# Two feed-forward norms through memory, and the last rows in tiles of 128 tokens

## The chip, the cores and the metric

The kernel runs on one core of one Trainium2 chip. The time is that of the device in microseconds; the kernel ran three times, and the median counts. Engines are called as in the profile: PE (TensorE), DVE (VectorE), ACT (ScalarE), POOL (GpSimd), SP (SyncE, which only issues transfers).

## The reference

The trunk has two layers over 512 tokens of 1024 features, float32. Layer 0 mixes tokens with a gated delta rule, layer 1 with latent attention. After each mixer comes a feed-forward network, and at the end one more norm:

```python
def rms_norm(x, gain):
    y = x * lax.rsqrt(jnp.mean(x * x, axis=-1, keepdims=True) + NORM_EPS)
    return y * gain

for i in range(2):
    x = x + mixer_i(rms_norm(x, norm_mix[i]))
    x = x + swiglu(rms_norm(x, norm_ffn[i]), w_gate_up[i], w_down[i])
return rms_norm(x, final_norm)

def swiglu(h, w_gate_up, w_down):      # 1024 -> 2 x 2816 -> 1024
    gu = h @ w_gate_up
    return (jax.nn.silu(gu[..., :D_FF]) * gu[..., D_FF:]) @ w_down
```

## The kernel before

**Layout.** Between the stages the tokens lie along the free axis: `xT` is 8 tiles of 128 features x 512 tokens. A dense product takes 128 columns of a weight matrix (a "unit", 512 KB, loaded by SP into `wst`). The unit is split into a high and a low part, `whi` (ACT, L122) and `wlo` (DVE, L123), in two halves of 128x512, and each of its eight slices is multiplied three times (`mm3`, L189 to L191), so 24 matmuls with 512 columns a unit. There is room for two split units and three loaded ones: a half of a unit is split when PE has used up the same half of the unit two before it.

**The feed-forward norm.** The factor of a token, 1/sqrt(mean of squares + eps), is not applied to the input of the network but to its products. While the gate and up products of the first of 22 feature tiles run on the tokens without their factor, the squares are already summed over the feature tiles in `acc`. `norm_scale` is called after the first gate and up product: `token_sum` (L209) sums `acc` over the partitions on PE, which leaves the sum of token t*128+p in partition p, column t; `rstd` computes the factor `r` (L202 on DVE, L203 on POOL, a power of -0.5). `spread` then makes `rb`, 128 partitions x 512 tokens with the factor of each token in every partition: DVE makes a diagonal matrix from `r` (L215), PE multiplies a matrix of ones with it (L218), ACT copies the result from PSUM (L220). `rb` is used at once: DVE multiplies the gate product by it (L861), ACT takes SiLU (L862), DVE multiplies by the up product (L863); then the result is split for the down product. L861 is also what frees the PSUM buffer of the gate product. The gate products use two buffers, `mm`; the up products use `st` and `sm` in turn. The down products use `rb` as well (L876). `norm_scale` runs twice, once in each layer; the norms of the attention call `spread` themselves.

**The end.** In the last layer, the down product of the last of eight feature tiles is taken by `last_rows` in two halves of 256 tokens. Its three weight units are split ahead. Behind each half the new `xT` is made (L907, L909), squared (L911) and multiplied by the gain (L913); PE sums the squares over the partitions for each of two tiles of 128 tokens (L917, L918) and turns the tile (L919); `rstd` makes the factor for both; DVE and ACT scale the rows in `y_rows` (L923 to L927), and SP and ACT send them, one 512 KB transfer for 128 tokens (L928).

**Order of the work.** The framework sets semaphores and orders the instructions of each engine itself: an instruction that its planner takes to be ready goes ahead of a waiting one of earlier code, so splits of later units stand between the steps of the norm. Each engine then executes in this order: whatever stands behind a waiting instruction waits as well. `after(first, then)` fixes the order of two instructions; `ordered` pins PE's order in the scan and the attention, not in the feed-forward networks.

Of the kernel before, what the change touches and what calls it, by code (L numbers as in the profile page):

```python
# [11 lines left out]
F32 = mybir.dt.float32  # L12
F32R = mybir.dt.float32r
I32 = mybir.dt.int32
AF = mybir.ActivationFunctionType
ALU = mybir.AluOpType
AX = mybir.AxisListType

P = 128
T = 512  # L20
D = 1024
# [29 lines left out]
def tile_trunk(ctx, tc, x, positions, norm_mix, norm_ffn, gdn_w_in, gdn_conv_w, gdn_a_log,  # L51
# [4 lines left out]
    act, dve, pe, pool, sync = nc.scalar, nc.vector, nc.tensor, nc.gpsimd, nc.sync  # L56
# [5 lines left out]
    sp = ctx.enter_context(tc.tile_pool(name="sp", bufs=2))  # L62
    pp = ctx.enter_context(tc.tile_pool(name="pp", bufs=2, space=bass.MemoryType.PSUM))
    dp = ctx.enter_context(tc.tile_pool(name="dp", bufs=1, space=bass.MemoryType.DRAM))
# [3 lines left out]
    def psum(tag, shape=(P, T)):  # L68
        return pp.tile(list(shape), F32, name="ps_" + tag, tag=tag, bufs=PS_BUFS[tag])

    def temp(shape, dtype=F32):
        return sp.tile(list(shape), dtype, name="temp", tag="t2", bufs=T2_BUFS)

    def slot(shape, tag, dtype=F32):
        return bp.tile(list(shape), dtype, name="slot_" + tag, tag=tag)


    ident = cp.tile([P, P], F32, name="ident")
    make_identity(nc, ident)
    ones = cp.tile([P, P], F32, name="ones")  # L80
# [36 lines left out]
    def gain(row):  # L117
        return gains[:, row:row + 1]
# [7 lines left out]
    def after(first, then):  # L126
        tc.add_manual_dep(then.ins, first.ins.name, mybir.DependencyInfo(
            mybir.DependencyClass.NoSync, mybir.DependencyReason.DATA))
# [4 lines left out]
    def pin(ins):  # L133
        if ordered["on"]:
            if ordered["last"] is not None:
                after(ordered["last"], ins)
            ordered["last"] = ins
        return ins
# [33 lines left out]
    def weights():  # L172
        while order and len(loaded) + len(parted) < 3:
            load_next()
        while loaded and len(parted) < 2:
            split_next()
        return parted.pop(0)
# [15 lines left out]
    def dense(o, w, nk, rh, rl, k0=0, start=True, stop=True):  # L193
        for k in range(nk):
            last = mm3(o, w[0][k], w[1][k], rh[k0 + k], rl[k0 + k],
                       start and k == 0, stop and k == nk - 1)
        return last

    def rstd(ssq, n, scale):
        ms = sp.tile([P, 4], F32, name="ms", tag="ms")  # L200
        r = sp.tile([P, 4], F32, name="r", tag="rs", bufs=3)
        dve.tensor_scalar(ms[:, :n], ssq, scale, EPS, op0=ALU.mult, op1=ALU.add)  # L202
        pool.tensor_tensor(r[:, :n], ms[:, :n], neghalf[:, :n], op=ALU.pow)  # L203
        return r

    def token_sum(acc):
        ps = psum("aa")
        for t in range(4):
            pin(pe.matmul(ps[:, t:t + 1], lhsT=acc[:, t * P:(t + 1) * P], rhs=ones[:, 0:1],  # L209
                          start=True, stop=True))  # L210
        return ps[:, 0:4]

    def spread(r):
        diag = temp([P, 4, P])
        dve.tensor_tensor(diag, ident.unsqueeze(1).broadcast_to([P, 4, P]),  # L215
                          r.unsqueeze(2).broadcast_to([P, 4, P]), op=ALU.mult)
        ps = psum("aa")
        pin(pe.matmul(ps, lhsT=ones, rhs=diag.rearrange("p a b -> p (a b)"), start=True, stop=True))  # L218
        rb = sp.tile([P, T], F32, name="rb", tag="rb", bufs=2)
        act.activation(rb, ps, AF.Copy)  # L220
        return rb
# [9 lines left out]
    def new_acc():  # L231
        return sp.tile([P, T], F32, name="acc", tag="acc", bufs=1)
# [6 lines left out]
    def gained(h, kt, src, row):  # L239
        act.activation(h[0][kt], src, AF.Copy, scale=gain(row))  # L240
        return dve.scalar_tensor_tensor(h[1][kt], src, gain(row), h[0][kt].bitcast(F32),
                                        op0=ALU.mult, op1=ALU.subtract)
# [6 lines left out]
    D2, scaled = D // 2, []  # L249
    for t in range(4):  # L250
# [3 lines left out]
        else:  # L254
# [3 lines left out]
                op0=ALU.mult, op1=ALU.add, accum_out=ssq[:, 1, t:t + 1]))  # L258
            dve.tensor_tensor(total, total, ssq[:, 1, t:t + 1], op=ALU.add)
        with tc.issue_after(scaled[t - 1].ins) if t in (1, 2) else ExitStack():  # L260
            r = rstd(total, 1, 1.0 / D)
# [7 lines left out]
    for k in range(KT):  # L269
        last = gained(h, k, banks[k], k)  # L270
# [472 lines left out]
    def scan(g, ready, late, between):  # L743
        for c in range(NCH):
            (bdp, bdq), vb, ks, rr = ready
            after_this = (g, c + 1) if c < NCH - 1 else (1, 0) if g == 0 else None
            vps = products(bdp, rr, "sm")
            vn = temp([P, GH, P])
            for p in range(2):
                act.activation(pairs(vn, p), pairs(vps, p), AF.Copy)  # L750
            if late is not None:
                scan_out(*late)
            if c < NCH - 1:
                advance(c, ks, vn)
            if after_this:
                mats = load_chunk(*after_this)
                vb = turn_values(*after_this)
            o_c = oc[:, c % 2]
            ops = products(bdq, vn, "aa")
            if c:  # L760
                dve.tensor_tensor(o_c, o_c, ops, op=ALU.add)
            else:
                act.activation(o_c, ops, AF.Copy)
            if after_this:
                ks = turn_keys(*after_this)
                ready = mats, vb, ks, recall(g, c + 1, vb) if c < NCH - 1 else vb
            late = scan_norm(g, c, o_c)
            between(c)
        return ready, late
# [12 lines left out]
    xT = slot([P, KT, T], "z0")  # L782
# [31 lines left out]
    _, late = scan(1, ready, late, second_half)  # L814
# [16 lines left out]
    acc = new_acc()  # L831
# [12 lines left out]
    def ffn(gain_row, rb, aside=None):  # L844
# [36 lines left out]
        if gain_row is None:  # L881
            last_rows(mh, ml, rb)
# [10 lines left out]
    def last_rows(mh, ml, rb):  # L893
        spare = slot([P, 4, KT, P], "h_lo", F32R)
        room.extend((spare[:, 2 * i, k:k + WK], spare[:, 2 * i + 1, k:k + WK])
                    for i in range(2) for k in range(0, KT, WK))
        m = KT - 1
        ws = [weights() for _ in DOWN]
        for half in range(2):
            ts = slice(half * T // 2, (half + 1) * T // 2)  # L900
            ps = psum("mm")
            o = ps[:, 0:T // 2]
            for (k0, nk), w in zip(DOWN, ws):
                dense(o, w, nk, [t[:, ts] for t in mh], [t[:, ts] for t in ml], k0=k0,
                      start=k0 == 0, stop=k0 == 15)
            t = temp([P, T // 2])
            dve.tensor_tensor(t, o, rb[:, ts], op=ALU.mult)  # L907
            y = xT[:, m, ts]
            dve.tensor_tensor(y, y, t, op=ALU.add)  # L909
            sq = temp([P, T // 2])  # L910
            act.activation(sq, y, AF.Square)  # L911
            g = temp([P, T // 2])
            dve.tensor_scalar(g, y, gain(32 + m), None, op0=ALU.mult)  # L913
            pt, pn = psum("sm"), psum("aa")
            for i in range(2):
                cs = slice(i * P, (i + 1) * P)
                pe.matmul(pn[:, i:i + 1], lhsT=acc[:, ts][:, cs], rhs=ones[:, 0:1], start=True, stop=False)  # L917
                pe.matmul(pn[:, i:i + 1], lhsT=sq[:, cs], rhs=ones[:, 0:1], start=False, stop=True)  # L918
                pe.transpose(pt[:, cs], g[:, cs], ident)  # L919
            r = rstd(pn[:, 0:2], 2, 1.0 / D)  # L920
            for i in range(2):
                tt = 2 * half + i
                dve.tensor_scalar(y_rows[:, tt, m * P:], pt[:, i * P:(i + 1) * P], r[:, i:i + 1], None, op0=ALU.mult)  # L923
                if i:
                    act.activation(y_rows[:, tt, :m * P], y_rows[:, tt, :m * P], AF.Copy, scale=r[:, i:i + 1])
                else:
                    dve.tensor_scalar(y_rows[:, tt, :m * P], y_rows[:, tt, :m * P], r[:, i:i + 1], None, op0=ALU.mult)  # L927
                (act if i else sync).dma_start(out[0, tt * P:(tt + 1) * P, :], y_rows[:, tt])  # L928

    def norm_scale():  # L930
        return spread(rstd(token_sum(acc), 4, 1.0 / D))

    mla = ExitStack()
    mp = mla.enter_context(tc.tile_pool(name="mp", bufs=2, reuse_waits="tile"))
# [3 lines left out]
    def rotary_tables():  # L938
# [28 lines left out]
        act.activation(sinT, sinT, AF.Sin, scale=freq[:, 1:2])  # L967

    ffn(8, norm_scale, rotary_tables)


# [42 lines left out]
    r = rstd(token_sum(acc), 4, 1.0 / D)  # L1014
# [8 lines left out]
    r = rstd(token_sum(qacc), 4, 1.0 / (QR * P))  # L1023
# [128 lines left out]
    r = rstd(token_sum(kvacc), 4, 1.0 / (KVR * P))  # L1152
# [7 lines left out]
    for half_ in range(2):  # L1160
# [4 lines left out]
        for t in range(4):  # L1165
            ps = psum("sm" if t % 2 else "st")
            ts = slice(t * P, (t + 1) * P)
# [71 lines left out]
    acc = new_acc()  # L1239
    for m in range(KT):  # L1240
# [3 lines left out]
        finish(m, 24)  # L1244
    y_rows = slot([P, 4, D], "h_hi")
    ffn(None, norm_scale)


# [20 lines left out]
```

## Time and profile before

| | us |
|---|---|
| median of 3 runs | 1454.41 |
| lowest and highest | 1453.83, 1454.73 |
| the profiled execution, its own time | 1455.12 |
| its span in the trace, first to last instruction | 1453.3 |
| PE busy in the span | 1417.8 |
| DVE busy in the span | 818.5 |
| ACT busy in the span | 587.5 |

The profiled execution is one of its own, so a row of its trace belongs to 1455.12 us, not to the median. Times in rows are microseconds from the start of the span. Busy times of matmuls overlap, since they are pipelined: their starts tell PE's pace.

### The profile page before, as it was taken

The numbers are of one execution on the slowest core, as the hardware profiler recorded it, in microseconds if no ns is written. First come the engines' busy times: TensorE is split into PE (matmuls) and PEld (weight loads), VectorE is DVE, ScalarE is ACT, GpSimd is POOL, SyncE is SP. The second block draws the span as 40 slices with busy tenths as digits, with TensorE's granted clock in tenths as the row PEclk, the third lists the DMA queues.
The fourth block names the chain that finished last, engine by engine and source line by source line (L and its number), as shares of the span: only waits on it lengthen the run. The fifth ranks groups of instructions, "written<-read, shape, count | busy, mean of one in ns | idle before, by whom it ended". The sixth has DMA issues, their size and how long they took to land.

```text
span 1453.3 us, 19974 instructions
## 1 busy us (share of the span) xinstructions
PE 1417.8 (98%) x7729; PEld 1181.7 (81%) x7729; DVE 818.5 (56%) x1367; ACT 587.5 (40%) x1139; POOL 111.7 (8%) x138
## 2 busy tenths in 40 slices
PE   7999999999999999999999999899999999999997
PEld 5788877788888888888888888688888888888887
DVE  6669984677877646444444444766654444443332
ACT  6643433332424433333333233487634333333332
POOL 2212000021221000000000000321000000000000
PEclk9999999999999999999999999999999999999999
DMA  5545449322421333333333333224133333233331
GB/s 154 138 129 144 113 131 199 70 61 63 122 63 51 91 95 98 101 101 89 100 98 92 93 101 83 65 74 107 54 92 101 89 101 101 88 99 92 94 93 71
DMA packets 274603, 141.91 MB, mean 98 GB/s; under 512 B 48510, under 2 KB 269868, under 8 KB 274124
## 3 DMA queue, kind: packets, MB, share of 16 engines
q1 hardware_dynamic: 270060, 128.96, 32.6%
q0 software_dynamic: 3808, 10.50, 2.4%
q8 instruction: 61, 1.00, 0.3%
q10 hardware_dynamic: 640, 1.18, 0.2%
q14 instruction: 34, 0.28, 0.1%
HBM read 128.47 MB, written 8.98 MB: 95 GB/s over the span
## 4 chain that ended last, share of the span: by engine, by line
PE 91%; DVE 4%; ACT 2%; issue 2%; POOL 0%; DMA 0%; SPq 0%; POOLq 0%; DVEq 0%; ACTq 0%
PE ps_mm L189 19%; PE ps_mm L190 19%; PE ps_mm L191 18%; PE ps_st L189 5%; PE ps_st L191 5%; PE ps_st L190 5%; PE ps_sm L189 3%; PE ps_sm L190 3%; PE ps_sm L191 3%; PE ps_aa L677 2%; PE ps_st L700 1%; PE ps_sm L388 1%; PE ps_aa L693 1%; PE ps_sm L693 1%; PE ps_sm L656 1%
## 5 line engine op out<-in xcount | busy, mean ns | idle before, releaser
L122 ACT ACTIVATE whi<-wst 128x512 fp32r<-128x512 f32 (+2 forms) x458 | 274.8, 604 | 633.8 <-PE ps_mm L190 416.4
L123 DVE TENSOR_TENSOR wlo<-wst,whi 128x512 fp32r<-128x512 f32 (+2 forms) x426 | 291.2, 685 | 321.6 <-ACT whi L122 313.2
L189 PE MATMUL ps_mm<-h_hi,whi 128*128 128x512 f32 x640 | 254.8, 398 | 0.0
L190 PE MATMUL ps_mm<-h_lo,whi 128*128 128x512 f32 x640 | 250.8, 392 | 0.0
L191 PE MATMUL ps_mm<-h_hi,wlo 128*128 128x512 f32 x640 | 250.7, 392 | 0.0
L190 PE MATMUL ps_mm<-slot_v,whi 128*128 128x512 f32 (+1 forms) x440 | 169.7, 386 | 0.0
L189 PE MATMUL ps_mm<-slot_q,whi 128*128 128x512 f32 (+1 forms) x384 | 148.8, 388 | 0.0
L191 PE MATMUL ps_mm<-slot_q,wlo 128*128 128x512 f32 (+1 forms) x384 | 148.4, 387 | 0.0
L189 PEld LDWEIGHTS ps_mm<-h_hi,whi 128*128 128x128 f32 x640 | 121.3, 190 | 27.4 <-issue 2.3
L191 PEld LDWEIGHTS ps_mm<-h_hi,wlo 128*128 128x128 f32 x640 | 120.9, 189 | 25.9
L190 PEld LDWEIGHTS ps_mm<-h_lo,whi 128*128 128x128 f32 x640 | 121.1, 189 | 25.2 <-issue 1.0
L189 PE MATMUL ps_st<-h_hi,whi 128*128 128x512 f32 x320 | 125.5, 392 | 0.0
L190 PE MATMUL ps_st<-h_lo,whi 128*128 128x512 f32 x320 | 124.8, 390 | 0.0
L191 PE MATMUL ps_st<-h_hi,wlo 128*128 128x512 f32 x320 | 124.8, 390 | 0.0
L190 PEld LDWEIGHTS ps_mm<-slot_v,whi 128*128 128x128 f32 x440 | 82.7, 188 | 16.5 <-DVE slot_v L123 0.2
L189 PEld LDWEIGHTS ps_mm<-slot_q,whi 128*128 128x128 f32 x384 | 72.2, 188 | 14.9 <-issue 1.0
L191 PEld LDWEIGHTS ps_mm<-slot_q,wlo 128*128 128x128 f32 x384 | 72.1, 188 | 14.2
L203 POOL TENSOR_TENSOR r<-ms,neghalf 128x4 f32<-128x4 f32 (+2 forms) x11 | 10.5, 954 | 890.5 <-DVE ms L202 870.8
L191 PEld LDWEIGHTS ps_st<-h_hi,wlo 128*128 128x128 f32 x320 | 60.2, 188 | 12.6
L189 PEld LDWEIGHTS ps_st<-h_hi,whi 128*128 128x128 f32 x320 | 60.0, 188 | 12.4
L190 PEld LDWEIGHTS ps_st<-h_lo,whi 128*128 128x128 f32 x320 | 60.1, 188 | 12.3
L189 PE MATMUL ps_sm<-h_hi,whi 128*128 128x512 f32 x176 | 68.5, 389 | 0.0
(365 smaller groups left out, 2149.2 us busy)
## 6 DMA issues: line engine op xcount, KB each, us to landing
wst<-in_ffn_w_gate_up SPq DMA_DIRECT2D x88, 512.0 KB, 3.9
wst<-in_gdn_w_in SPq DMA_DIRECT2D x48, 512.0 KB, 5.8
wst<-in_ffn_w_down SPq DMA_DIRECT2D x32, 448.0 KB, 3.7
wst<-in_gdn_w_out SPq DMA_DIRECT2D x16, 512.0 KB, 4.3
wst<-in_ffn_w_down SPq DMA_DIRECT2D x16, 512.0 KB, 4.0
wst<-in_mla_w_out SPq DMA_DIRECT2D x8, 512.0 KB, 4.9
wst<-in_mla_w_in SPq DMA_DIRECT2D x5, 512.0 KB, 4.0
wst<-in_mla_w_q_up SPq DMA_DIRECT2D x8, 288.0 KB, 3.1
```

The lines of the kernel that those rows point to most:

```text
L122: act.activation(hi, src, AF.Copy)
L123: return eng.tensor_tensor(lo, src, hi.bitcast(F32), op=ALU.subtract)
L189: pin(pe.matmul(o, lhsT=ah, rhs=bh, start=start, stop=False))
L190: pin(pe.matmul(o, lhsT=ah, rhs=bl, start=False, stop=False))
L191: return pin(pe.matmul(o, lhsT=al, rhs=bh, start=False, stop=stop))
L203: pool.tensor_tensor(r[:, :n], ms[:, :n], neghalf[:, :n], op=ALU.pow)
L388: pe.matmul(ps[:, c * CH:(c + 1) * CH], lhsT=qkh[kh][:, c].rearrange("p a b -> p (a b)"), rhs=qkh[kh][:, c, 1], start=True, stop=True)
L656: pin(pe.transpose(ps[:, k * P:(k + 1) * P], vs[g][:, k, c].rearrange("p a b -> p (a b)"), ident))
L677: pin(pe.matmul(both[z][half(hh), k * P:(k + 1) * P], lhsT=qks[g][:, k, c, z], rhs=S[:, 2 * k + hh], start=True, stop=True))
L693: pin(pe.matmul(ps[:, k * P:(k + 1) * P], lhsT=lhs[:, k], rhs=rhs[:, k], start=True, stop=True))
L700: pin(pe.matmul(st[:, k * P:(k + 1) * P], lhsT=ks[half(hh), k], rhs=vn[half(hh), k], start=True, stop=True))
```

## The change

`norm_scale` no longer calls `spread`, but `cast_wide`: POOL issues a transfer that writes the four columns of `r` to a 4 x 128 array in device memory, in the order of the tokens, and then one that reads this row of 512 numbers into all 128 partitions of `rb`. The attention's norms keep `spread`.

In `last_rows` the product of a half stays in one piece of 256 columns. The steps behind it are done for each 128 tokens: the scaling by `rb` and the addition on DVE, with the second tile ordered behind the first; the squares on ACT; the gain, on ACT now instead of DVE; two `rstd` of one column instead of one of two columns; the transposes behind the sums; and DVE scales the first 896 columns of the first tile before its last 128.

```diff
--- before.py
+++ after.py
@@ -903,32 +903,46 @@
             for (k0, nk), w in zip(DOWN, ws):
                 dense(o, w, nk, [t[:, ts] for t in mh], [t[:, ts] for t in ml], k0=k0,
                       start=k0 == 0, stop=k0 == 15)
-            t = temp([P, T // 2])
-            dve.tensor_tensor(t, o, rb[:, ts], op=ALU.mult)
-            y = xT[:, m, ts]
-            dve.tensor_tensor(y, y, t, op=ALU.add)
-            sq = temp([P, T // 2])
-            act.activation(sq, y, AF.Square)
-            g = temp([P, T // 2])
-            dve.tensor_scalar(g, y, gain(32 + m), None, op0=ALU.mult)
             pt, pn = psum("sm"), psum("aa")
-            for i in range(2):
-                cs = slice(i * P, (i + 1) * P)
+            cols = [slice(i * P, (i + 1) * P) for i in range(2)]
+            ys = [xT[:, m, ts][:, cs] for cs in cols]
+            for i, (cs, y) in enumerate(zip(cols, ys)):
+                t = temp([P, P])
+                scaled = dve.tensor_tensor(t, o[:, cs], rb[:, ts][:, cs], op=ALU.mult)
+                if i:
+                    after(added, scaled)
+                added = dve.tensor_tensor(y, y, t, op=ALU.add)
+            sqs, gs = [temp([P, P]) for _ in ys], [temp([P, P]) for _ in ys]
+            for sq, y in zip(sqs, ys):
+                act.activation(sq, y, AF.Square)
+            for g, y in zip(gs, ys):
+                act.activation(g, y, AF.Copy, scale=gain(32 + m))
+            for i, cs in enumerate(cols):
                 pe.matmul(pn[:, i:i + 1], lhsT=acc[:, ts][:, cs], rhs=ones[:, 0:1], start=True, stop=False)
-                pe.matmul(pn[:, i:i + 1], lhsT=sq[:, cs], rhs=ones[:, 0:1], start=False, stop=True)
-                pe.transpose(pt[:, cs], g[:, cs], ident)
-            r = rstd(pn[:, 0:2], 2, 1.0 / D)
-            for i in range(2):
+                pe.matmul(pn[:, i:i + 1], lhsT=sqs[i], rhs=ones[:, 0:1], start=False, stop=True)
+            rs = [rstd(pn[:, i:i + 1], 1, 1.0 / D) for i in range(2)]
+            for i, cs in enumerate(cols):
+                pe.transpose(pt[:, cs], gs[i], ident)
+            for i, (cs, r) in enumerate(zip(cols, rs)):
                 tt = 2 * half + i
-                dve.tensor_scalar(y_rows[:, tt, m * P:], pt[:, i * P:(i + 1) * P], r[:, i:i + 1], None, op0=ALU.mult)
+                head, last = y_rows[:, tt, :m * P], y_rows[:, tt, m * P:]
                 if i:
-                    act.activation(y_rows[:, tt, :m * P], y_rows[:, tt, :m * P], AF.Copy, scale=r[:, i:i + 1])
+                    act.activation(head, head, AF.Copy, scale=r[:, 0:1])
                 else:
-                    dve.tensor_scalar(y_rows[:, tt, :m * P], y_rows[:, tt, :m * P], r[:, i:i + 1], None, op0=ALU.mult)
+                    dve.tensor_scalar(head, head, r[:, 0:1], None, op0=ALU.mult)
+                dve.tensor_scalar(last, pt[:, cs], r[:, 0:1], None, op0=ALU.mult)
                 (act if i else sync).dma_start(out[0, tt * P:(tt + 1) * P, :], y_rows[:, tt])
 
+
+    def cast_wide(r):
+        d = dp.tile([4, P], F32, name="r_d")
+        pool.dma_start(d.rearrange("t p -> p t"), r[:, 0:4])
+        rb = sp.tile([P, T], F32, name="rb", tag="rb", bufs=2)
+        pool.dma_start(rb, bass.AP(tensor=d.tensor, offset=d.offset, ap=[[0, P], [1, T]]))
+        return rb
+
     def norm_scale():
-        return spread(rstd(token_sum(acc), 4, 1.0 / D))
+        return cast_wide(rstd(token_sum(acc), 4, 1.0 / D))
 
     mla = ExitStack()
     mp = mla.enter_context(tc.tile_pool(name="mp", bufs=2, reuse_waits="tile"))
```

## Rows read from the trace of the kernel before

**Rows 1.** The page, part 1 (busy, share, instructions) and part 4 (chain).

```profile
PE 1417.8 (98%) x7729; PEld 1181.7 (81%) x7729; DVE 818.5 (56%) x1367; ACT 587.5 (40%) x1139; POOL 111.7 (8%) x138
...
PE 91%; DVE 4%; ACT 2%; issue 2%; POOL 0%; DMA 0%; SPq 0%; POOLq 0%; DVEq 0%; ACTq 0%
```

**Rows 2.** Timeline, PE, first norm: start, length, line, [idle before].

```profile
534.43 0.40 PE L191 MATMUL ps_mm<-h_hi,wlo 128*128 128x512 f32 x1
535.40 1.12 PE L218 MATMUL ps_aa<-temp,ones 128*128 128x512 f32 x2 [0.57 <-DVE temp L215]
...
536.59 0.39 PE L190 MATMUL ps_mm<-h_lo,whi 128*128 128x512 f32 x1
...
545.91 0.39 PE L189 MATMUL ps_mm<-h_hi,whi 128*128 128x512 f32 x1
```

**Rows 3.** Timeline of PE, second norm.

```profile
1088.46 0.40 PE L191 MATMUL ps_mm<-h_hi,wlo 128*128 128x512 f32 x1
1089.52 1.10 PE L218 MATMUL ps_aa<-temp,ones 128*128 128x512 f32 x2 [0.67 <-DVE temp L215]
...
1090.69 0.40 PE L190 MATMUL ps_mm<-h_lo,whi 128*128 128x512 f32 x1
```

**Rows 4.** Timeline of POOL, then of DVE, first norm.

```profile
533.61 1.01 POOL L203 TENSOR_TENSOR r<-ms,neghalf 128x4 f32<-128x4 f32 x1 [63.66 <-DVE ms L202]
...
537.19 0.69 DVE L861 TENSOR_TENSOR temp<-ps_mm,rb 128x512 f32<-128x512 f32 x1 [1.25 <-ACT rb L220]
538.38 0.69 DVE L123 TENSOR_TENSOR wlo<-wst,whi 128x512 fp32r<-128x512 f32 x1 [0.50 <-ACT whi L122]
```

**Rows 5.** Timeline of POOL, early: a write and a read of kk_d.

```profile
37.36 0.98 POOL L382 DMA_DIRECT2D kk_d<-temp  x1 [22.66 <-ACT temp L381]
40.33 0.62 POOL L370 DMA_DIRECT2D slot_z<-kk_d  x1 [1.99 <-DMA kk_d<-temp]
```

**Rows 6.** DMA view, us to landing; last, queue 0 at 44 to 47 us.

```profile
wst<-in_mla_w_q_up SPq DMA_DIRECT2D x8, 288.0 KB, 3.1
...
slot_z<-kk_d POOLq DMA_DIRECT2D x8, 256.0 KB, 8.9
...
kk_d<-temp POOLq DMA_DIRECT2D x8, 128.0 KB, 5.2
...
q0 software_dynamic: 8, 0.13, 10.2%
```

**Rows 7.** Timeline of SP's queue and DVE: load of the positions.

```profile
547.43 0.37 SPq L148 DMA_DIRECT2D wst<-in_ffn_w_gate_up  x1
547.85 0.57 SPq L940 DMA_DIRECT2D temp<-in_positions  x1
...
552.76 0.42 DVE L946 CAST temp<-temp 128x512 f32<-128x512 int32 x1
```

**Rows 8.** Timeline: POOL at 12 us, DVE at 1426 us, the end.

```profile
11.96 0.55 POOL L203 TENSOR_TENSOR r<-ms,neghalf 128x1 f32<-128x1 f32 x1 [1.19 <-DVE ms L202]
...
1426.44 0.69 DVE L876 TENSOR_TENSOR temp<-ps_mm,rb 128x512 f32<-128x512 f32 x1 [2.56 <-PE ps_mm L191]
...
1443.88 0.42 DVE L907 TENSOR_TENSOR temp<-ps_mm,rb 128x256 f32<-128x256 f32 x1 [4.46 <-PE ps_mm L191]
...
1444.80 0.42 ACT L911 ACTIVATE temp<-slot_z 128x256 f32<-128x256 f32 x1 [5.54 <-DVE slot_z L909]
...
1445.80 0.36 PE L918 MATMUL ps_aa<-ones,temp 128*128 128x1 f32 x2
...
1446.44 0.70 POOL L203 TENSOR_TENSOR r<-ms,neghalf 128x2 f32<-128x2 f32 x1 [8.27 <-DVE ms L202]
1447.17 1.04 ACT L925 ACTIVATE slot_h_hi<-slot_h_hi,r 128x896 f32<-128x896 f32 x1 [1.96 <-POOL r L203]
...
1447.44 0.68 DVE L927 TENSOR_SCALAR slot_h_hi<-slot_h_hi,r 128x896 f32<-128x896 f32 x1
...
1448.46 0.34 ACTq L928 DMA_DIRECT2D out_y<-slot_h_hi  x1
```

## The prediction, made before the changed kernel was run

> **What bounds the kernel.** I read the page's busy times and chain first: PE is busy for 98% of the span, and the chain that ended last runs through PE for 91% of it [rows 1]. So an edit counts if it takes time out of PE's stream, or out of the tail after PE's last product, and costs nothing where PE has other work. The edit touches three places: the two feed-forward norms, and the last rows.
>
> The timeline of PE at the first norm shows the price of the old spreading. One product of the dense run starts at 534.43; then PE waits 0.57 us for the diagonal matrix that DVE makes (L215), and runs the two passes of L218. The next product is hidden behind them, and the one after it starts at 536.59 [rows 2]. The reader should see three products' starts that are 2.16 us apart where two steps would do. One step is 0.227 us: from the product at 536.59 to the first one of the third gate product, at 545.91, are 41 steps in 9.32 us [rows 2]. The second norm has the same picture, 1088.46 to 1090.69, 2.23 us [rows 3].
>
> **Part 1, taken out.** In both norms the diagonal on DVE, PE's two passes and ACT's copy go. On PE that is 2.16 - 2 x 0.227 = 1.70 us in the first norm and 2.23 - 0.45 = 1.77 us in the second, its wait for DVE included: 3.47 us. In this stretch PE goes from product to product without idle time up to 545.91 [rows 2], so what it no longer does moves everything behind it, if nothing new stops it.
>
> **Part 1, added: the round trip.** POOL's power ends at 533.61 + 1.01 = 534.62 [rows 4]. Then POOL issues a write of 128 x 4 numbers, each to a place of its own, waits for it, and issues a read that gives all 128 partitions the same 2 KB row (256 KB). No such pair is in the trace, so I bound it.
>
> The write: the nearest row is kk_d's, also on POOL's queue, also in 512 pieces (128 partitions, 4 rows of 64 numbers each), 256 bytes a piece. Its issue began at 37.36 and the transfer that waited for it was issued at 40.33, 2.97 us [rows 5]. The eight of them take 5.2 us at the median [rows 6], with other transfers in the way. In the norm POOL has nothing else in flight, so I take 3.0; bounds 2.97 and 5.2.
>
> The read: 288 KB loads land after 3.1 us [rows 6]. The positions are the same pattern, one 2 KB row to 128 partitions: issued at 547.85, used by DVE at 552.76, so at most 4.9 us, and that one was issued just behind a 512 KB weight load [rows 7]. I take 4.0; bounds 3.1 and 4.9.
>
> So rb stands at 534.62 + 3.0 + 4.0, about 541.7, where it was there at 537.19 before [rows 4].
>
> Of this pair the Trainium skill (DMA: Bandwidth & Descriptors, Rules for kernel authors) says that a last dimension that isn't contiguous becomes one descriptor for each element and should be rearranged, and the same page's Specifications say that pieces under 512 bytes cost a read and a write; that speaks against this write. By it the write would be 512 tiny descriptors; the kk_d row has as many pieces, also under 512 bytes, and took 2.97 us, so I leave the sum as it is.
>
> **What waits for rb.** L861 on DVE (gate times rb), behind it SiLU on ACT, and behind both, in their queues, the weight splits of later units: the next `wlo` stands right behind L861, at 538.38 [rows 4]. PE needs two things from this for its third gate product: the buffer of the first one (there are two "mm" buffers, and L861 is what empties it), and the next weights. That product started at 545.91 and moves to 545.91 - 1.70 = 544.21. L861 takes 0.69 [rows 4]; with one split of 0.69 behind it and 0.05 of handing over, rb must be there by about 542.8. That is 8.2 us after the power; my pair takes 7.0. So I cost the round trip at nothing: the first up product and the second unit's two products cover it. With 1.2 us less cover, each further microsecond costs one in each norm. The second norm has the same work in the same order around it. The write and read on POOL hold up nobody else: POOL's next work is in the mixer, far behind.
>
> **Part 2, the last rows.** The products stay as they are (256 columns a half). Only the steps behind them are cut in two. In the first half they lie beside PE's second half; PE executes the same number of small products, so I cost it at nothing (if that cover went, a tail of the size below). In the second half they are the end of the kernel. I step from 1443.88, when DVE starts L907 [rows 8].
>
> A DVE step costs 0.69 for 512 columns and 0.42 for 256 [rows 8], so about 0.29 for 128. Two pairs of them, one behind the other and slightly overlapped, end near 1445.03; before, the Square behind the one pair started at 1444.80. The second Square (0.42 for 256 columns, so 0.31 for 128) then ends at 1445.37 instead of 1445.22 [rows 8]. But PE's last small product then comes at once: the other ones wait for nothing late and the transposes stand behind it. Before, it started at 1445.80, 0.58 after the Square's end, and took 0.36 [rows 8]; now I expect it to end at 1445.83 instead of 1446.16. The power goes from one of 128x2, 0.70, to two of 128x1, 0.55 each [rows 8]. With 0.28 for the step on DVE between (1446.16 to 1446.44 in [rows 8]) the first factor is there at 1446.66 (before 1447.14), the second at 1447.21.
>
> DVE does the 896 columns of tile 2 (0.68) and its last 128 (0.29 as above), so SP can send it near 1447.65, where DVE's 0.68 ended at 1448.12 before [rows 8]: 0.48 earlier. ACT scales tile 3 after the second factor, 1.04 us, to 1448.28, and issues near 1448.33; before, at 1448.46 [rows 8]: 0.13 earlier. ACT's two new gain steps end near 1446.1, before it is wanted. The two transfers share the engines, so the end lies between -0.13 and -0.48; I take 0.4. Bounds: if each 128x1 power took the 1.01 of the 128x4 one [rows 4], the second factor is 0.92 later and the tail loses up to 0.8; at best it gains 0.6.
>
> **Sum.** 1.70 + 1.77 + 0.4 = 3.87 us off. The profiled execution took 1455.12 us by its own clock (span 1453.3 and 1.8 around it), so 1451.25 for a like one. The median of the runs is 0.71 below that execution: **1450.5 us**, 0.27% less. A difference of 0.2%, 2.9 us, is about what a measurement of this kernel can tell from no change.
>
> **Rivals.**
>
> *The factor comes late.* Both transfers at their upper bounds, 5.2 + 4.9 = 10.1 us, is 1.9 more than the cover, in each norm: PE stands still for 3.8 us in all and the gain is gone but for 0.1, so 1454.3. For it: kk_d's median, and weight loads every few microseconds that share the engines. Against it: the quiet kk_d row and POOL's empty queue. Anything between it and my forecast is this rival in part. Chance 0.25.
>
> *The read runs on few engines (slower).* The reads of kk_d and qk_d on POOL's queue are also 256 KB, and land after 8.9 us [rows 6]. While the first of them runs alone, its queue uses 10.2% of the 16 engines' time [rows 6], less than two of them. If a read that repeats one row is spread as badly, the pair takes 2.97 + 8.9 = 11.9 us, 3.7 over the cover, and 7.4 in two norms: 1455.12 - 3.87 + 7.4 - 0.71 = 1457.9. It decides for slower than before from a pair of 10.1 us on. By the Trainium skill (DMA: Bandwidth & Descriptors, Rules for kernel authors) the slowest dimension sets the number of engines, and a leading repeat of c copies below 16 confines a transfer to c of them. The trace agrees with it for kk_d, whose pattern starts with a repeat of two; here the leading repeat is 128, so by that rule this rival falls. Chance 0.10.
>
> *The tail loses.* Two powers, one behind the other on POOL, cost more than the smaller tiles save: by the bound above 0.8 lost instead of 0.4 gained, so 1451.7, just inside no change. Against it: the 0.55 row. Chance 0.05.
>
> **Chances and range.** My forecast 0.60, the three rivals 0.40. Faster by over 0.2% means below 1451.5: the forecast, 0.60. Slower by over 0.2% means above 1457.3: the few-engines rival and the end of the late factor's, 0.11. Within: 0.29. The range takes the forecast with the best tail and the spread of the runs of before (0.5 each way) at its low end, 1449.6, and the late factor at its bounds at its high end, 1454.4; it leaves out the slower rival and little else. The forecast's own range is 1449.6 to 1451.6.
>
> **What the profile after should show.** L218, L215 and ACT's L220 gone from both norms, and no idle PE from the sums of tokens to the third gate product. POOL: the write within 0.1 us of the power, the read some 3 us later. L861's wait named after the transfer into rb, ending about 7 us after the power. The third gate product about 1.7 us earlier relative to the sums of tokens. At the end two 128x1 powers, and SP's last send half a microsecond nearer to the last product. I am wrong if PE's third gate product waits for DVE (L861) or for ACT's and DVE's splits: then the pair took more than 8.2 us. I am wrong on the tail if ACT's send is issued later than 4.6 us after the second half's L907 started (1443.88 to 1448.46 in [rows 8]).

## The result, and the profile after

| | before | after |
|---|---|---|
| median, 6 runs each | 1454.56 us | 1464.83 us |
| lowest and highest | 1453.83, 1456.29 | 1461.49, 1465.83 |
| ratio after/before, 95% interval | | 1.0067 (1.0056 to 1.0079) |
| the profiled execution, its span | 1455.12, 1453.3 | 1461.49, 1459.8 |

The change made the kernel 10.3 us slower; 3.9 us faster was forecast, and the time lies above the whole range. The profiled execution of after is the lowest of its six, so the two profiles differ by 6.5 us only; where the rest is, is said below.

The page of after, parts 1 and 4 as in [rows 1], and the group of part 5 that changed (count, busy us, mean ns, then idle time ahead of it and what ended it):

```profile
PE 1417.2 (97%) x7725; PEld 1182.1 (81%) x7725; DVE 816.8 (56%) x1369; ACT 587.6 (40%) x1143; POOL 116.6 (8%) x144
...
PE 85%; issue 6%; DVE 4%; ACT 2%; DMA 2%; POOL 1%; POOLq 0%; SPq 0%; DVEq 0%; ACTq 0%
...
L189 PE MATMUL ps_mm<-h_hi,whi 128*128 128x512 f32 x640 | 255.6, 399 | 9.5 <-DVE temp L861 9.5
```

PE has the work of before, less the four passes of L218, and DMA stands on the chain with 2%. The 6% of "issue" are not lost time: 63.6 us of them are POOL's idle time ahead of the first power, which the chain counts there. The new thing is the last line: PE stood still for 9.5 us, waiting for L861.

The timeline of POOL in both norms, against [rows 4] (start, length, line, [idle before <- what ended it]):

```profile
531.69 1.39 POOL L203 TENSOR_TENSOR r<-ms,neghalf 128x4 f32<-128x4 f32 x1 [63.67 <-DVE ms L202]
533.37 0.86 POOL L939 DMA_DIRECT2D r_d<-r  x1 [0.29 <-POOL r L203]
541.26 0.57 POOL L941 DMA_DIRECT2D rb<-r_d  x1 [7.04 <-DMA r_d<-r]
...
1088.73 1.39 POOL L203 TENSOR_TENSOR r<-ms,neghalf 128x4 f32<-128x4 f32 x1 [85.58 <-DVE ms L202]
1091.29 0.82 POOL L939 DMA_DIRECT2D r_d<-r  x1 [1.17 <-issue]
1099.71 0.57 POOL L941 DMA_DIRECT2D rb<-r_d  x1 [7.60 <-DMA r_d<-r]
```

From the issue of the write to that of the read that waits for it: 7.89 us in the first norm, 8.42 in the second. The forecast had 3.0. The write itself was issued 0.29 and 1.17 us after the power, where 0.1 was expected. The timeline of DVE shows when the read was there:

```profile
545.17 0.69 DVE L861 TENSOR_TENSOR temp<-ps_mm,rb 128x512 f32<-128x512 f32 x1 [9.72 <-DMA rb<-r_d]
...
1104.55 0.69 DVE L861 TENSOR_TENSOR temp<-ps_mm,rb 128x512 f32<-128x512 f32 x1 [12.06 <-DMA rb<-r_d]
```

So the read took 3.9 and 4.8 us, between the forecast's bounds. PE's timeline, against [rows 2, 3], from the sums of tokens to the third gate product and behind it:

```profile
530.46 0.95 PE L209 MATMUL ps_aa<-ones,acc 128*128 128x1 f32 x8
...
542.06 0.39 PE L191 MATMUL ps_sm<-h_hi,wlo 128*128 128x512 f32 x1
546.01 0.76 PE L189 MATMUL ps_mm<-h_hi,whi 128*128 128x512 f32 x1 [3.57 <-DVE temp L861]
546.58 0.63 PE L190 MATMUL ps_mm<-h_lo,whi 128*128 128x512 f32 x1
547.00 0.63 PE L191 MATMUL ps_mm<-h_hi,wlo 128*128 128x512 f32 x1
...
552.27 0.39 PE L189 MATMUL ps_mm<-h_hi,whi 128*128 128x512 f32 x1
...
1087.50 0.95 PE L209 MATMUL ps_aa<-ones,acc 128*128 128x1 f32 x8
...
1099.10 0.39 PE L191 MATMUL ps_sm<-h_hi,wlo 128*128 128x512 f32 x1
1105.39 0.77 PE L189 MATMUL ps_mm<-h_hi,whi 128*128 128x512 f32 x1 [5.91 <-DVE temp L861]
...
1108.66 0.39 PE L191 MATMUL ps_mm<-h_hi,wlo 128*128 128x512 f32 x1
```

Two losses stand here. One is the wait: the third gate product would have started one step of 0.227 behind 542.06, so it is 3.72 us late, and 6.06 in the second norm. The other stands behind the wait: the steps are 0.43 us. From 546.01 to 552.27 are 15 steps in 6.26 us, 2.86 more than at 0.227; from 1105.39 to 1108.66 are 8 steps, 1.45 more. The windows of the first norm show what goes with it (start and end of a stretch in us, its length, busy us of PE, PEld (PE's weight loads), DVE, ACT and POOL, then granted clock of PE, DMA share, GB/s):

```profile
530.00:545.00 15.00, 12.44 (x59) 10.10 (x57) 1.45 (x3) 1.89 (x3) 2.81 (x3) 1.00 0.24 54
545.00:546.00 1.00, 0.00 (x0) 0.02 (x1) 0.82 (x2) 0.10 (x1) 0.00 (x0) 0.56 0.00 0
546.00:551.00 5.00, 4.99 (x12) 3.94 (x13) 4.28 (x8) 3.35 (x6) 0.00 (x0) 0.50 0.37 107
551.00:552.00 1.00, 1.00 (x4) 0.81 (x3) 0.77 (x2) 0.63 (x1) 0.00 (x0) 0.53 0.06 18
552.00:560.00 8.00, 8.00 (x37) 6.60 (x37) 4.87 (x10) 2.12 (x4) 0.00 (x0) 1.00 0.56 163
```

After PE had stood still, its granted clock was 0.50 (1.2 GHz) and came back to 1.00 (2.4 GHz) 6 us later. That the standing still brings the low clock is tried in e7.

What was taken out is gone, as forecast. PE's timeline of before has the sums of both norms and the third gate product of the second:

```profile
532.38 0.95 PE L209 MATMUL ps_aa<-ones,acc 128*128 128x1 f32 x8
...
1086.41 0.95 PE L209 MATMUL ps_aa<-ones,acc 128*128 128x1 f32 x8
...
1099.99 0.39 PE L189 MATMUL ps_mm<-h_hi,whi 128*128 128x512 f32 x1
```

Without the lateness, 542.06 + 0.23 - 530.46 = 11.83 us lie between sums and third gate product, where before 13.53 did (532.38 to 545.91 in [rows 2]): 1.70 less. In the second norm 1099.10 + 0.23 - 1087.50 = 11.83 stand against 1099.99 - 1086.41 = 13.58: 1.75 less.

The end, against [rows 8]: first SP's send of before, then, of after, the second half's scaling, the two powers, both sends.

```profile
1448.14 0.36 SPq L928 DMA_DIRECT2D out_y<-slot_h_hi  x1
...
1450.85 0.29 DVE L911 TENSOR_TENSOR temp<-ps_mm,rb 128x128 f32<-128x128 f32 x1 [4.50 <-PE ps_mm L191]
...
1453.05 1.31 POOL L203 TENSOR_TENSOR r<-ms,neghalf 128x1 f32<-128x1 f32 x2 [7.17 <-DVE ms L202]
...
1454.61 0.36 SPq L934 DMA_DIRECT2D out_y<-slot_h_hi  x1
1455.46 0.34 ACTq L934 DMA_DIRECT2D out_y<-slot_h_hi  x1
```

From the first DVE step to the end of the span are 1459.8 - 1450.85 = 8.95 us; before 1453.3 - 1443.88 = 9.42. The tail gains 0.47. ACT's send stands 4.61 us behind the first step (before 4.58), SP's 3.76 (before 4.26). From SP's send to the end of the span are 5.19 us, 5.16 before and 5.16 in e2, so the end moved with SP's send and not with ACT's.

**The balance.** First norm -1.70 + 3.72 + 2.86 = +4.88; second -1.75 + 6.06 + 1.45 = +5.76; tail -0.47: +10.2 us, against +10.27 by the medians. The two profiled executions show +6.5, because in stretches that the edit doesn't touch the one of after was 1.9 us ahead already when the first norm began and gained another 1.9 between the norms. The granted clock was higher there in the run of after (1.00 against 0.98 in the first 100 us, 0.97 against 0.95 from 200 to 300, 0.98 against 0.97 from 900 to 1000); the runs of before themselves lie up to 8 us apart (1448.59 to 1456.66 in a later session, with mean clocks of 0.996 and 0.990). That the 3.8 us are such differences between executions is argued from these clocks; those stretches were not tried any further.

### The profile page after: what moved, and what is told of

Read it like the earlier page. It is cut to its first block, busy times and chain, and to the rows that moved or that the text cites. A ratio compares the mean times of both kernels' runs of the same rounds, so it can differ in the third digit from the quotient of the medians.

```text
span 1459.8 us, 19987 instructions
## 1 busy us (share of the span) xinstructions
PE 1417.2 (97%) x7725; PEld 1182.1 (81%) x7725; DVE 816.8 (56%) x1369; ACT 587.6 (40%) x1143; POOL 116.6 (8%) x144
## 3 DMA queue, kind: packets, MB, share of 16 engines
HBM read 129.00 MB, written 8.98 MB: 95 GB/s over the span
## 4 chain that ended last, share of the span: by engine, by line
PE 85%; issue 6%; DVE 4%; ACT 2%; DMA 2%; POOL 1%; POOLq 0%; SPq 0%; DVEq 0%; ACTq 0%
PE ps_mm L189 18%; PE ps_mm L190 17%; PE ps_mm L191 17%; PE ps_st L189 5%; PE ps_st L191 5%; PE ps_st L190 5%; PE ps_sm L189 3%; PE ps_sm L190 3%; PE ps_sm L191 3%; PE ps_aa L677 2%; PE ps_st L700 1%; DMA r_d<-r 1%; PE ps_sm L388 1%; PE ps_aa L693 1%; PE ps_sm L693 1%
## 5 line engine op out<-in xcount | busy, mean ns | idle before, releaser
L189 PEld LDWEIGHTS ps_mm<-h_hi,whi 128*128 128x128 f32 x640 | 121.7, 190 | 37.2 <-issue 12.1
L203 POOL TENSOR_TENSOR r<-ms,neghalf 128x1 f32<-128x1 f32 (+1 forms) x13 | 12.5, 966 | 880.2 <-DVE ms L202 860.4
L861 DVE TENSOR_TENSOR temp<-ps_mm,rb 128x512 f32<-128x512 f32 x44 | 30.4, 691 | 81.8 <-PE ps_mm L191 60.0
```

Source lines behind the costliest of these rows:

```text
L189: pin(pe.matmul(o, lhsT=ah, rhs=bh, start=start, stop=False))
L861: dve.tensor_tensor(g, pg, rb, op=ALU.mult)
```

## The experiments

Two questions were open: whether all of the loss comes from the norms, and why the write takes 8 us where kk_d's 512 pieces took 2.97 [rows 5]. The profile gives a first hint. The DMA view of after, from 535 to 537 us and from 537 until the read is issued:

```profile
q0 software_dynamic: 32, 0.00, 8.5%
...
DMA packets 0, 0.00 MB, mean 0 GB/s; under 512 B 0, under 2 KB 0, under 8 KB 0
```

All 32 packets of the write are through by 537 us. Then no queue moves anything for 4.2 us, and the write still isn't reported complete. The time doesn't go into moving its 2 KB, as far as the packets in the trace show it. By the Trainium skill (DMA: Bandwidth & Descriptors, Anatomy of one DMA) most of a transfer's fixed time of some 2 us is the wait until memory has confirmed the last byte. The trace agrees that such a wait is the larger part, but not with its size: here that wait alone is over 4 us. So the theories are on the side of memory: the pieces of 4 bytes lie side by side in one small block and are slow to complete because of that (the first theory), or the number of pieces counts, or the place of the write in the kernel.

**e1: part 1 alone.**

```diff
...
     def norm_scale():
-        return spread(rstd(token_sum(acc), 4, 1.0 / D))
+        return cast_wide(rstd(token_sum(acc), 4, 1.0 / D))
```

> The two norms through memory alone, the last rows as before. Theory A (the write of 512 pieces of 4 bytes completes some 8 us after its issue instead of my 3.0; PE waits for L861 and then runs at the lower clock for a while): all of the loss is here, so about 10.7 us over the kernel before (1465.3), 0.4 more than the changed kernel, since the tail's gain is missing; the trace shows 7 to 9 us from the write's issue to the read's in both norms, and PE idle 3 us or more before the third gate product. Rival (the loss comes from the last rows or from an order changed elsewhere): within 0.2% of before.

Measured: 1465.18 us (4 runs) against 1453.72 of before (19), ratio 1.0079 (1.0057 to 1.0101). Write to read 8.87 us in the first norm, 9.04 in the second; PE stood still for L861 for 11.5 us in all. The loss, 11.5 us by the medians, is that of the norms; it is 0.8 more than expected, with a longer write and a longer wait than in after.

**e2: part 2 alone** (`norm_scale` as before, `last_rows` as after).

> The last rows in tiles of 128 tokens alone, the norms through the product as before. Theory A: 0.45 us under before (1454.1), read from the trace as 8.95 us from the second half's first scaling to the end of the span instead of 9.42, and no other difference. Rival (the change in the last rows costs something that the faster end hides): at least 0.5 us over before.

Measured: 1453.54 us (10 runs), ratio 0.9998 (0.9986 to 1.001). In its trace 8.98 us lie between the first step of the second half and the end of the span, 0.44 less than the 9.42 of before. The gain is in the trace; the times can't tell it from nothing.

**e3: the write in 128 pieces of 16 bytes.** Memory holds the four numbers of a partition side by side, so the write is one piece for each partition; DVE puts the order of tokens right by reading `rb` with a step of 16 bytes, in L861, L876 and `last_rows`.

```diff
...
-        d = dp.tile([4, P], F32, name="r_d")
-        pool.dma_start(d.rearrange("t p -> p t"), r[:, 0:4])
+        d = dp.tile([P, 4], F32, name="r_d")
+        pool.dma_start(d, r[:, 0:4])
...
-        return rb
+        return rb.rearrange("q (p t) -> q t p", t=4)
```

> The changed kernel with the factors written in the order in which they lie, 4 numbers of a partition side by side: 128 pieces of 16 bytes instead of 512 of 4, the memory row and the read the same size; DVE reads rb with a step of 4 numbers. Theory A1 (the scattered 4-byte pieces make the write slow to complete): the read is issued 3 to 4 us after the write, rb is there in time, no PE idle: 1450.6, 0.27% under before. Rival A2 (any write to memory from this place completes only after some 8 us, whatever its pieces, for example behind the weight load that runs beside it): 8 us as in the changed kernel, and 1464.

Measured: 1450.12 us (10 runs) against 1453.72, ratio 0.9972 (0.9959 to 0.9985): 3.6 us faster than before, the only kernel here that is faster than before clear of the noise. POOL's timeline in both norms, then DVE's and PE's in the first:

```profile
529.72 0.65 POOL L939 DMA_DIRECT2D r_d<-r  x1 [0.29 <-POOL r L203]
532.86 0.56 POOL L941 DMA_DIRECT2D rb<-r_d  x1 [2.50 <-DMA r_d<-r]
...
1082.22 0.60 POOL L939 DMA_DIRECT2D r_d<-r  x1 [0.29 <-POOL r L203]
1085.14 0.55 POOL L941 DMA_DIRECT2D rb<-r_d  x1 [2.32 <-DMA r_d<-r]
...
536.39 1.06 DVE L861 TENSOR_TENSOR temp<-ps_mm,rb 128x512 f32<-128x512 f32 x1 [4.59 <-DMA rb<-r_d]
...
526.81 0.95 PE L209 MATMUL ps_aa<-ones,acc 128*128 128x1 f32 x8
...
538.63 0.39 PE L189 MATMUL ps_mm<-h_hi,whi 128*128 128x512 f32 x1
```

Write to read is 3.14 and 2.92 us, the figure that the prediction had. PE's third gate product comes without idle time 11.82 us behind the sums, 1.71 less than before. L861 takes 1.06 us instead of 0.69 with the step; PE doesn't wait for it.

**e4: the write measured by itself.** On the kernel before, five small writes stand on POOL's queue beside the first network's down products, each followed by a read that waits for it, twice over. Nothing else uses them. The table is from one execution.

```diff
...
+            d1 = dp.tile([4, P], F32, name="pr_close%d" % n)
+            pool.dma_start(d1.rearrange("t p -> p t"), s[:, 0:4])
+            pool.dma_start(s[0:4], d1[:, 0:16])
+            d2 = dp.tile([4, P, 16], F32, name="pr_apart%d" % n)
+            pool.dma_start(d2.rearrange("t p e -> p t e")[:, :, 0:1], s[:, 0:4].unsqueeze(2))
...
```

> The kernel before with a series of small writes to memory on POOL's queue beside the first network's down products, each followed by a short read that waits for it, twice over: 512 pieces of 4 bytes with neighbours side by side as in the change; 512 pieces of 4 bytes, each 64 bytes from the next; 128 pieces of 16 bytes; 512 pieces of 128 bytes; 128 pieces of 4 bytes. Theory A1 (pieces that share a small block of memory wait for each other): side by side 7 to 8 us from issue to the read's issue, 64 bytes apart about 3, 16-byte pieces about 3 to 4, 128-byte pieces 3, 128 pieces of 4 bytes 3 to 4. Rival B (it is the number of pieces under some size, wherever they lie): both kinds of 512 small pieces take 7 to 8, and the 128 of 4 bytes 3 to 4. Rival A2 (the place in the kernel): all five about equal.

Measured, us from issue to the issue of the read, first and second time:

| write | pieces | us |
|---|---|---|
| pr_close: as in the change | 512 of 4 bytes, side by side | 10.32, 10.34 |
| pr_apart | 512 of 4 bytes, 64 bytes apart | 2.56, 4.32 |
| pr_row: as in e3 | 128 of 16 bytes, side by side | 2.85, 3.21 |
| pr_wide | 512 of 128 bytes, side by side | 3.82, 4.33 |
| pr_one | 128 of 4 bytes, side by side | 8.38, 7.92 |

The two extremes in POOL's timeline:

```profile
778.51 0.86 POOL L937 DMA_DIRECT2D pr_close<-probe  x1 [246.21 <-DVE probe L934]
788.83 0.56 POOL L938 DMA_DIRECT2D probe<-pr_close  x1 [9.46 <-DMA pr_close<-probe]
795.41 0.80 POOL L940 DMA_DIRECT2D pr_apart<-probe  x1 [6.02 <-issue]
797.97 0.69 POOL L941 DMA_DIRECT2D probe<-pr_apart  x1 [1.76 <-DMA pr_apart<-probe]
```

The same 512 numbers from the same tile take 10.3 us side by side and 2.6 to 4.3 apart. So neither the place in the kernel nor the number of pieces by itself makes it slow (512 of 128 bytes are fast too). The first theory was wrong in one expectation: 128 pieces of 4 bytes should have taken 3 to 4 us and took 8. A quarter of the pieces saves a quarter of the time at most; how they lie decides.

**e5: the same, with the step alone changed**: 512 pieces of 4 bytes, 4, 8, 16, 32 and 64 bytes apart, on the kernel before.

```diff
...
+            for step in (1, 2, 4, 8, 16):
+                d = dp.tile([4, P, step], F32, name="pr_step%d_%d" % (step, n))
+                pool.dma_start(d.rearrange("t p e -> p t e")[:, :, 0:1], s[:, 0:4].unsqueeze(2))
+                pool.dma_start(s[0:4], d[:, 0:16, 0])
```

> The kernel before with small writes on POOL's queue as in the last probe, always 512 pieces of 4 bytes, but with a step from a piece to its neighbour in memory of 4, 8, 16, 32 and 64 bytes, each followed by a short read that waits for it, twice over. Theory A1 (pieces that share a block of some 64 bytes are written one behind the other): the time from the write's issue to the read's falls with the step, 10.3 us at 4 bytes, about 6.5 at 8, about 4.5 at 16, 3 to 4 at 32 and 64. Rival A3 (only writes that together fill whole blocks are slow, or a threshold): 10.3 at 4 bytes and 3 to 4 at every other step.

| step, bytes | 4 | 8 | 16 | 32 | 64 |
|---|---|---|---|---|---|
| first time, us | 10.62 | 5.07 | 3.43 | 2.51 | 3.09 |
| second time, us | 10.16 | 4.51 | 3.92 | 3.22 | 3.20 |

Two of these pairs in POOL's timeline, the first with a step of 4 bytes and the first with 8:

```profile
775.60 0.86 POOL L938 DMA_DIRECT2D pr_step<-probe  x1 [246.21 <-DVE probe L934]
786.22 0.56 POOL L939 DMA_DIRECT2D probe<-pr_step  x1 [9.76 <-DMA pr_step<-probe]
792.76 0.79 POOL L938 DMA_DIRECT2D pr_step<-probe  x1 [5.99 <-issue]
797.83 0.68 POOL L939 DMA_DIRECT2D probe<-pr_step  x1 [4.28 <-DMA pr_step<-probe]
```

The table is from one execution as well. The time more than halves with the first doubling of the step and from 16 or 32 bytes on stays near 3. It falls in steps, as the first theory had it, but faster: 5.1 and 4.5 at 8 bytes where 6.5 was expected, and 3.4 and 3.9 at 16 where 4.5 was. Only the step differs between these writes, so the nearness of small pieces is shown to be the cause. The write with a step of 4 bytes came first in its series both times, but in e4 the slow pr_one came last, so the place in the series doesn't explain it. That memory takes pieces of one block one behind the other would explain it, but this is argued from the table; what happens inside the memory was not seen.

The trace shows a side effect. The DMA view of e5 from 780 to 786 us, within the slow write, and from 805 to 811 us, as the write with a step of 32 bytes came to its end:

```profile
wst<-in_ffn_w_down SPq DMA_DIRECT2D x1, 448.0 KB, 9.4
...
wst<-in_ffn_w_down SPq DMA_DIRECT2D x1, 448.0 KB, 4.0
```

A weight load beside the slow write landed after 9.4 us instead of 4.0, and another after 9.2 beside the second one; in e4 it was 9.6 beside pr_close and 10.8 beside pr_one. PE did not wait for them there.

**e6: no round trip.** The product of `spread` is kept, but stands behind the second gate product, so that PE needn't wait for the diagonal; the last rows as in the change.

```diff
...
+            if m == 1:
+                rb = spread(rb)
+                tail(*held, rb)
...
     def norm_scale():
-        return spread(rstd(token_sum(acc), 4, 1.0 / D))
+        return rstd(token_sum(acc), 4, 1.0 / D)
```

> No trip through memory: the product of the norm stays on PE, but behind the second gate product instead of among its first steps, so that PE no longer waits for the diagonal matrix; the last rows in tiles of 128 tokens. If what PE lost in the two norms was its wait (0.57 and 0.67 us) and the passes of the product (1.13 and 1.10): 1.24 us for the waits and 0.45 for the tail less than before, 0.12%. If the order was not the cause of the wait: only the tail's 0.45, 0.03%.

Measured: 1451.19 us (10 runs) against 1453.55 (13), ratio 0.999 (0.9976 to 1.0004). L218 runs at 535.95 and 1089.32 with no idle time ahead of it, so the wait of 0.57 and 0.67 [rows 2, 3] is gone. From the sums to the third gate product PE takes 12.73 us in both norms, 0.80 and 0.85 less than before. The times agree with such a gain, but can't tell it from nothing.

**e7: what the wait does to the clock.** The change as it is, with 14 products that nobody uses (labelled L862) ahead of the third gate product, where PE waits.

```diff
...
+            if m == 1:
+                idle = psum("aa")
+                for k in range(14):
+                    mm = pe.matmul(idle, lhsT=h[0][k % KT][:, 0:P], rhs=h[0][k % KT], start=k == 0, stop=k == 13)
...
```

> The changed kernel, with 14 products of 512 columns that nobody uses put on PE between the second up product and the third gate product of each network (3.2 us at the full clock), where PE stood idle for 3.57 and 5.91 us. Theory (PE's lower clock behind the wait comes from its standing idle): the products fall into the wait, the third gate product starts no later, and it runs at the higher clock for most of its steps: 2.9 and 1.5 us less, so 3 to 4.3 us under the changed kernel, 1460 to 1461. Rival (the lower clock has another cause, or the products move everything behind them): as the changed kernel, or up to 6.4 us more.

PE's timeline, both norms (here L868 is the step that was L861):

```profile
538.91 3.33 PE L862 MATMUL ps_aa<-h_hi 128*128 128x512 f32 x14
543.40 0.47 PE L189 MATMUL ps_mm<-h_hi,whi 128*128 128x512 f32 x1 [1.16 <-DVE temp L868]
...
1103.43 0.47 PE L189 MATMUL ps_mm<-h_hi,whi 128*128 128x512 f32 x1 [2.62 <-DVE temp L868]
...
1104.89 0.57 PE L189 MATMUL ps_mm<-h_hi,whi 128*128 128x512 f32 x1
...
1105.69 0.63 PE L191 MATMUL ps_mm<-h_hi,wlo 128*128 128x512 f32 x1
```

In the first norm PE stood still for 1.16 us, the granted clock stayed at 1.00, and the steps behind were 0.23: the 2.86 us of after are not there. In the second it stood still for 2.62 us, and 1.5 us behind the wait the clock fell to 0.50 for a while: 16 steps in 5.34 us, 1.71 too many. So one of the two losses was avoided. Measured: 1460.82 us (4 runs) against 1453.55, ratio 1.0067 (1.0043 to 1.0091). The medians lie 7.3 us apart, where those of after and before lie 10.3; the interval of the ratio holds both, so the times settle nothing here, and the median lies where it was expected although only one loss went. That the low clock belongs to the wait rests on the steps in the trace, and is shown for the first norm. The second, where 2.62 us of waiting were left and the clock still fell, agrees with it but doesn't test it.

## Why the prediction was wrong

- **Removed: 1.70 + 1.77 us.** Right: 1.70 and 1.75 were measured, and e3 gives 1.71 for the first norm.
- **"The write: ... I take 3.0; bounds 2.97 and 5.2."** This step failed. It took 7.9 and 8.4 us, and 8.9 and 9.0 in e1. The nearest row was chosen by the number of pieces and the queue. Neither of them settles it: in e4 writes of 512 pieces on this same queue took from 2.6 to 10.3 us. What matters is that pieces of 4 bytes lie side by side, and kk_d's of 256 bytes [rows 5] can't show that. The bound from below was sound; the one from above was a row of another kind. By the Trainium skill (DMA: Bandwidth & Descriptors, Specifications), pieces under 512 bytes cost a read and a write. The prediction weighed that and set it aside on the kk_d row; it pointed the right way, but by itself it doesn't tell these writes apart: pr_apart's pieces and pr_wide's are under 512 bytes too and took 2.6 to 4.3 us.
- **The start of the write.** The power took 1.39 us, not 1.01, and the write was issued 0.29 and 1.17 us behind it, not within 0.1. From the end of the power to L861 that makes 0.29 + 7.89 + 3.91 = 12.1 us in the first norm and 1.17 + 8.42 + 4.84 = 14.4 in the second, where 7.0 was forecast.
- **The read: 4.0 us.** Right: 3.9 and 4.8. With it falls the mechanism of the few-engines rival: the read was not slow. The slower end came by the write instead. The rival's point of decision, a pair of 10.1 us, holds: 12.1 and 14.4 us are over it, and the kernel is slower.
- **The cover: 8.2 us.** Right in size, in part by luck: the pair is 3.9 and 6.2 us over it, and the third gate product was 3.72 and 6.06 late, so 8.4 us were covered. No weight split stood between: the product started 0.84 us after L861 began, where the prediction allowed 1.43, while the longer power took 0.38 of the cover away. "Each further microsecond costs one in each norm" was too cheap: behind the wait PE ran at 1.2 GHz for a while, another 2.86 and 1.45 us, a term that the prediction didn't have. It is 4.3 of the 14.1 us that the change lost.
- **The late factor.** It named the right place, with bounds of 10.1 us that were too low.
- **The tail: 0.4 us.** Right in size: 0.47 in the trace of after, 0.44 in e2. SP's send came 0.50 us earlier, where 0.48 was forecast. ACT's came 0.03 later, where 0.13 earlier was forecast, because the two powers took 1.31 us and not 2 x 0.55; at 4.61 us it is just past the prediction's own sign of being wrong, 4.6. That cost nothing, since the end followed SP's send. With 1.31 and not the 2 x 1.01 of the bound, the rival of the losing tail falls.
- **The sum.** With a write of 3.0 it would have been right in size: e3 has 2.9 to 3.1 us and runs 3.6 us faster than before, where 3.87 was forecast.

## What to carry to other kernels

Before a round trip through memory is costed by a row of another transfer, compare how the pieces lie in memory, not only how many there are: write each partition's numbers as one piece, and let the reader put the order right, at the price that its step has (L861 in e3). When PE's cover might not last, price the wait at more than its length: the products behind it may run at half the clock, as they did here for some 6 and 3 us. Where a chain hangs on one transfer, look in the DMA view whether its packets are still moving or its completion is awaited; the two have different remedies.

## What the runs showed of the hardware

- 512 neighbouring pieces of 4 bytes took 7.9 to 10.6 us to be complete in device memory, 128 of them 7.9 to 8.4. In after no packet moved in the 4.2 us before the read was issued. With a step of 32 or 64 bytes it was 2.5 to 3.2 us in e5.
- Such a write held up other transfers: four weight loads of 448 KB landed after 9.2 to 10.8 us beside it (e4, e5), others of that size in the same stretches after 3.6 to 5.0.
- POOL's power of 128x4 took 1.39 us in after, where a weight split of DVE ran beside its first 0.5 us, and 1.01 in [rows 4], where DVE stood still for all of it.
- DVE's product with `rb` (L861) took 1.06 us with a step of 16 bytes in `rb` (e3) instead of 0.69.
- In the second norm of after POOL issued the write 1.17 us after the power, in the first 0.29, with nothing in the profile that it waited for; with 128 pieces (e3) it was 0.29 in both.
